# A hybrid decoder trunk on one core: the framework's scheduler orders the instructions by its timeline simulation of all engines in place of its simple one

## The chip, the cores and the metric

The kernel runs on one core of a Trainium2 chip. The core has five engines with an instruction queue each: TensorE (PE, matmuls; its weight loads are PEld in the profile), VectorE (DVE), ScalarE (ACT), GpSimd (POOL) and SyncE (SP, which issues the DMAs). An engine runs its queue in order, and semaphores hold an instruction until those of other engines that it needs are done. The metric is the time of one execution on the device in microseconds; lower is better.

## The reference

A trunk of four layers on 256 tokens of width 1024, in float32. Each layer adds half an FFN, a mixer and half an FFN; the mixer of layer i is i mod 3.

```python
def swiglu(h, w_gu, w_down):
    gate, up = jnp.split(h @ w_gu, 2, axis=-1)
    return (jax.nn.silu(gate) * up) @ w_down

for i in range(DEPTH):                      # DEPTH = 4
    kind, j = i % N_MIXERS, i // N_MIXERS
    x = x + 0.5 * swiglu(rmsnorm(x, ffn1_norm[i]), ffn1_w_gu[i], ffn1_w_down[i])
    h = rmsnorm(x, mix_norm[i])
    if kind == 0:   m = gated_deltanet(h, ...)          # layers 0 and 3
    elif kind == 1: m = stick_breaking_attention(h, ...)  # layer 1
    else:           m = dsa_sparse_attention(h, ...)      # layer 2
    x = x + m
    x = x + 0.5 * swiglu(rmsnorm(x, ffn2_norm[i]), ffn2_w_gu[i], ffn2_w_down[i])
return rmsnorm(x, final_norm)
```

The FFN is 1024 to 2 x 2816 and back. The gated DeltaNet projects to q, k, v, a gate z and two numbers per head, runs a short causal convolution and silu over q, k and v, normalises q and k, and solves, per head and chunk of tokens, a unit lower triangular system (`triangular_solve(lower + eye, rhs)`); a state is carried from chunk to chunk; the result is normalised, multiplied by silu(z) and projected back. Stick-breaking attention has 8 heads and log-sigmoid weights in place of a softmax. The sparse attention scores keys with an indexer, keeps the top 64 for each query and attends to those.

## The kernel before

The activations stay in SBUF with features on the partitions, x as 8 tiles of 128 x 256. Weights come in chunks of 128 x 2048 float32 (1 MB) by DMA. Every product is made of three matmuls in the fp32r type: each weight piece of 128 x 512 is split into a high part `h` (ScalarE, L172) and a low part `l` (VectorE, L173), and so are the activations (`xh`, `xl` at L224 and L225; `ah`, `al` at L201 and L202); `mm3` multiplies h by h, l by h and h by l (all matmuls are at L43, transposes at L56). A tile of an in-projection is 48 such matmuls into one PSUM bank, `bankG`; there are four banks under the tag G and four under the tag A. The ten buffers each of `h` and `l` set how far ahead weights can be split.

The program is written by `Trunk`, stage by stage. `ffn` runs 11 steps of two gate/up chunks and one down chunk. Its norm is folded in late: `norm_in` scales x by the gains, and `rstd` sums the squares (`ones,sq` matmuls), takes the inverse square root on VectorE in three Newton steps (`rs_y`, `rs_t`, L212 to L214), spreads it by two transposes (`ident,rs_y`) and copies it to `rb` (ScalarE, L261). What multiplies a tile by `rb` can start only then.

`gdn` is the DeltaNet stage. Sixteen in-projection tiles (kind 0 keys, 1 values, 2 queries, 3 the gate z; four groups `c` of two heads each) go through TensorE in the order of `gdn_order`. Beside them run generators, which write their next instructions whenever a hand-made clock (`now`, `due`, `pump`) says so: `gates` (exponentials and logarithms on ScalarE, then `E`), `keys(c)` (transposes of `kT`, its norm `rs_y`, `kT x kT`, the matrix `LL`, and then the inverse), `values`, `queries` and `delta(c)`. The inverse of a group doubles its block size in six levels, each of which is a strand of steps that wait for each other:

```python
b1.mm(blk(one(b1.t, r)), Ah[:, r], half(X, 0)[:, r])                                  # XX,LL   PE
nc.vector.tensor_mul(r4(Y), r4(b1.t), lmask[:, lv, None, :].to_broadcast([P, 4, 64]))  # L528   DVE
b2.mm(one(b2.t, r), XT[:, r], one(Y, r))                                              # Y,XX    PE
nc.vector.tensor_sub(half(X, 0), half(X, 0), c4(b2.t))                                # L533   DVE
b3.mm(blk(one(b3.t, r)), X[:, r], self.identh...)                                     # hf,XX   PE
nc.scalar.activation(half(XT, 1), c4(b3.t), AF.Copy)                                  # L538   ACT
```

At its end stand a residual `R` (L546) and two corrections, which give `XF`. `delta` waits for the inverses of all four groups; then follow the output's norm, the gate (L641) and the out-projection (`bankG<-oh`), which adds to x.

`sb` projects v, then q and k head by head, and runs `attend(h)` beside them: scores, absolute value, exp, log (L717 to L719), `sh`/`sl`, the matmuls with `ntri`, exp (L730), `att,v`, and the split of the head's output; `out_proj` takes two heads a chunk. `dsa` has strands of its own (`factor` with `fac`, `index_scores`, `select`, `attend`).

ScalarE's functions lie in table sets. The framework adds a load wherever an operation's function isn't in the set that is loaded by then.

The text of the program isn't yet the order of the queues. The framework's tile scheduler takes the instructions with their dependencies and orders them again for every engine, assigns buffers and sets the semaphores. It is this scheduler that the change concerns.

## Time and profile before

| | before |
|---|---|
| median of 3 runs | 2086.28 us (2080.59 to 2100.09) |
| profiled execution | 2071.74 us, its span 2069.90 us |
| TensorE busy | 2006.7 us (97%) |
| VectorE busy | 1611.2 us (78%) |
| ScalarE busy | 1306.9 us (63%) |
| GpSimd busy | 160.6 us (8%) |
| mean granted TensorE clock | 0.995 |

The profile is one execution; its span goes from the first to the last instruction, and 1.84 us lie around it. Busy times of an engine add up the stretches in which at least one instruction of it runs. The first DeltaNet stage lies at about 188 to 382 us, the stick-breaking stage at 745 to 853 us, the sparse attention at 1228 to 1325 us and the second DeltaNet stage at 1684 to 1883 us; the rest are the eight FFNs.

### The profile page before, as it was taken

The page shows a single profiled execution, that of the slowest core. Times are in us where ns is not written, and L with a number is a line of the kernel's source. Part 1 is how long each engine was busy: PE and PEld are TensorE (multiplying, and loading weights), DVE is VectorE, ACT ScalarE, POOL GpSimd, SP SyncE. Part 2 cuts the span into 40 slices and gives each one's busy share as a digit, 9 for nine tenths or more (in the row PEclk, how much of TensorE's full clock was granted, in tenths as well). Part 3 has the DMA queues.
Part 4 walks back from the last instruction along what each step waited for, and adds up shares of the span by engine and source line. Part 5 has one row for each costly group of instructions (what it writes and reads, how often), then busy time and mean ns, then how long its engine had stood idle before and what let it go on. Part 6 is the DMA issues. An engine that isn't in the chain of part 4 may idle for free.

```text
span 2069.9 us, 43693 instructions
## 1 busy us (share of the span) xinstructions
PE 2006.7 (97%) x17578; PEld 1975.3 (95%) x17578; DVE 1611.2 (78%) x3456; ACT 1306.9 (63%) x2804; POOL 160.6 (8%) x145
## 2 busy tenths in 40 slices
PE   8999899999999999999999998999999998999998
PEld 8999889999999989999999996999999998899998
DVE  7778898866787776877787788877787788988776
ACT  6666776655666666665666664766666667766664
POOL 1001311100000010100010013100010013111000
PEclk9999999999999999999999999999999999999999
DMA  7555223555455554555555542455555542235552
GB/s 260 200 189 182 103 104 127 176 190 185 164 204 197 190 183 146 178 198 196 191 183 201 187 153 79 150 198 201 186 185 202 186 181 105 101 123 181 186 200 86
DMA packets 52619, 353.93 MB, mean 171 GB/s; under 512 B 6976, under 2 KB 7872, under 8 KB 10688
## 3 DMA queue, kind: packets, MB, share of 16 engines
q1 hardware_dynamic: 52128, 350.49, 47.8%
q8 instruction: 137, 2.24, 0.4%
q10 hardware_dynamic: 288, 0.66, 0.1%
q14 instruction: 66, 0.54, 0.1%
HBM read 350.07 MB, written 1.05 MB: 170 GB/s over the span
## 4 chain that ended last, share of the span: by engine, by line
PE 79%; DVE 15%; ACT 4%; issue 2%; POOL 0%; DMA 0%; SPq 0%; ACTq 0%; DVEq 0%; POOLq 0%
PE bankG L43 52%; PE bankA L43 26%; DVE l L173 6%; ACT x L224 1%; PE bankA L56 1%; DVE kT L470 1%; ACT h L172 1%; DVE x L225 1%; DVE rs_t L213 1%; DVE rs_y L214 1%; DVE x L306 1%; DVE rs_t L212 1%; DVE qT L470 0%; DVE e L334 0%; DVE vT L470 0%
## 5 line engine op out<-in xcount | busy, mean ns | idle before, releaser
L43 PE MATMUL bankG<-x,h 128*128 128x256 f32 x7008 | 1256.5, 280 | 10.0 <-ACT x L224 6.8
L173 DVE TENSOR_TENSOR l<-r,h 128x512 fp32r<-128x512 f32 x1328 | 938.2, 713 | 396.7 <-ACT h L172 395.3
L172 ACT ACTIVATE h<-r 128x512 fp32r<-128x512 f32 x1328 | 821.9, 626 | 573.5 <-PE bankG L43 329.6
L43 PEld LDWEIGHTS bankG<-x,h 128*128 128x128 f32 x7008 | 1079.4, 189 | 12.4 <-ACT x L224 7.1
L43 PE MATMUL bankG<-x,l 128*128 128x256 f32 x3504 | 977.5, 279 | 0.0
L43 PEld LDWEIGHTS bankG<-x,l 128*128 128x128 f32 x3504 | 661.9, 189 | 0.2
L43 PE MATMUL bankA<-al,h 128*128 128x256 f32 x1408 | 389.6, 277 | 0.0
L43 PE MATMUL bankA<-ah,h 128*128 128x256 f32 x1408 | 389.6, 277 | 0.0
L43 PE MATMUL bankA<-ah,l 128*128 128x256 f32 x1408 | 389.5, 277 | 0.0
L43 PEld LDWEIGHTS bankA<-al,h 128*128 128x128 f32 x1408 | 265.1, 188 | 0.1
L43 PEld LDWEIGHTS bankA<-ah,h 128*128 128x128 f32 x1408 | 264.3, 188 | 0.1
L43 PEld LDWEIGHTS bankA<-ah,l 128*128 128x128 f32 x1408 | 264.3, 188 | 0.0
L334 DVE TENSOR_TENSOR e<-e,bankG 128x256 f32<-128x256 f32 x352 | 145.3, 413 | 1.8 <-ACT e L333 1.8
L333 ACT ACTIVATE e<-bankG 128x256 f32<-128x256 f32 x352 | 133.7, 380 | 9.1 <-PE bankG L43 8.5
L247 POOL TENSOR_TENSOR sq<-sq 128x512 f32<-128x512 f32 x12 | 15.7, 1304 | 1454.7 <-ACT sq L246 1454.7
L346 DVE TENSOR_TENSOR e<-e,rb 128x512 f32<-128x512 f32 x176 | 119.6, 684 | 0.0
L201 ACT ACTIVATE ah<-e 128x256 fp32r<-128x256 f32 x176 | 72.8, 418 | 23.0 <-DVE e L348 22.7
L347 ACT ACTIVATE e<-e 128x256 f32<-128x256 f32 x176 | 71.2, 405 | 5.8 <-DVE e L346 5.8
L43 PE MATMUL bankG<-oh,h 128*128 128x256 f32 x256 | 73.4, 287 | 0.1
L348 DVE TENSOR_TENSOR e<-e 128x256 f32<-128x256 f32 x176 | 72.8, 418 | 0.5 <-ACT e L347 0.5
L202 DVE TENSOR_TENSOR al<-e,ah 128x256 fp32r<-128x256 f32 x176 | 72.7, 417 | 0.5 <-ACT ah L201 0.5
L43 PE MATMUL bankG<-oh,l 128*128 128x256 f32 x256 | 71.2, 279 | 0.0
(290 smaller groups left out, 1683.7 us busy)
## 6 DMA issues: line engine op xcount, KB each, us to landing
r<-in_ffn SPq DMA_DIRECT2D x262, 1024.0 KB, 4.8
r<-in_gdn_in SPq DMA_DIRECT2D x32, 1024.0 KB, 4.8
r<-in_gdn_out SPq DMA_DIRECT2D x8, 1024.0 KB, 4.7
r<-in_sb_qk SPq DMA_DIRECT2D x8, 1024.0 KB, 4.9
r<-in_sb_v SPq DMA_DIRECT2D x4, 1024.0 KB, 4.8
r<-in_sb_out SPq DMA_DIRECT2D x4, 1024.0 KB, 4.8
r<-in_dsa_out SPq DMA_DIRECT2D x4, 1024.0 KB, 4.8
r<-in_dsa_in SPq DMA_DIRECT2D x3, 1024.0 KB, 4.8
```

Source lines behind the costliest of these rows:

```text
L43: self.nc.tensor.matmul(out, lhsT, rhs, start=self.fresh, stop=stop, skip_group_check=True)
L56: self.nc.tensor.transpose(out, x, self.k.ident)
L172: self.nc.scalar.activation(h[:, :pw], src, AF.Copy)
L173: (self.nc.gpsimd if pool else self.nc.vector).tensor_sub(l[:, :pw], src, h[:, :pw].bitcast(F32))
L201: self.nc.scalar.activation(dh, src, AF.Copy)
L202: self.nc.vector.tensor_sub(dl, src, dh.bitcast(F32))
L212: nc.vector.tensor_mul(t, y, y)
L333: nc.scalar.activation(e[:, m * T:(m + 1) * T], b.t[:, :T], AF.Copy)
L334: nc.vector.tensor_add(e[:, m * T:(m + 1) * T], e[:, m * T:(m + 1) * T], b.t[:, T:])
L346: nc.vector.tensor_mul(e2, e2, st["rb"][:, None, :].to_broadcast([P, 2, T]))
L347: nc.scalar.activation(e[:, :T], e[:, :T], AF.Silu)
L348: nc.vector.tensor_mul(e[:, T:], e[:, T:], e[:, :T])
```

## The change

One argument, in `kernel()`:

```diff
-    with tile.TileContext(nc) as tc:
+    with tile.TileContext(nc, schedule_with_timeline_sim=True) as tc:
         trunk(tc, aps, out)
```

The scheduler now orders the instructions by a timeline simulation of all engines. The instructions of TensorE, VectorE, GpSimd and SyncE are the same. On ScalarE 16 table loads are added, 25 in place of 9: six in each DeltaNet stage, three in the stick-breaking stage and one behind it. Of TensorE's 18086 instructions 6663 stand elsewhere among the others (by up to 832 places), of VectorE's 1622, of ScalarE's 2476 (by at most 80). The middles of the FFNs are as before; what moves lies at the borders of the stages and in the mixers.

In a DeltaNet stage TensorE's in-projection tiles move ahead of the side work: of TensorE's places counted from the start of the program, the `ident,rs_y` transposes for `rb` go from 1684 to 1755, the gates' `gg` matmuls from 1733 to 1870, the first `kT` transposes from 1822 to 2017, the first `hf,XX` matmul of the inverse from 2005 to 2249, and the last of the 16 tiles ends at 2585, where it ended at 3360; the first out-projection matmul goes from 3360 to 3316.

On ScalarE in the first DeltaNet stage, the gates of the first layer before (L420 to L428 are steps of `gates`, each of which waits for the one ahead of it):

```order
L420 ACTIVATE beta<-bankA 128x4x2
L172 ACTIVATE h<-r 128x512
L424 ACTIVATE ge<-gz 128x16
L172 ACTIVATE h<-r 128x512
L425 ACTIVATE ge<-ge 128x16
L426 ACTIVATE ge<-ge,ones 128x16
L428 ACTIVATE ea<-ad 128x8
```

and now:

```order
L420 ACTIVATE beta<-bankA 128x4x2
L172 ACTIVATE h<-r 128x512
L673 ACT_TABLE_LOAD
L673 ACTIVATE z<-z 128x512
L424 ACTIVATE ge<-gz 128x16
L425 ACT_TABLE_LOAD
L425 ACTIVATE ge<-ge 128x16
L172 ACTIVATE h<-r 128x512
L426 ACT_TABLE_LOAD
L426 ACTIVATE ge<-ge,ones 128x16
L428 ACT_TABLE_LOAD
L428 ACTIVATE ea<-ad 128x8
```

The silu of the gate z (L673) has moved between the gates' own steps, and loads of the table sets stand around it; two more follow at the next z, among the exponentials of `E`.

On VectorE in the same stage, the rows up to the last `R` before (`XX` steps are the inverse's, `l` weight splits, `vT` and `pc` the convolution):

```order
L528 TENSOR_TENSOR Y<-bankA,tab 128x256
L173 TENSOR_TENSOR l<-r,h 128x512
L533 TENSOR_TENSOR XX<-XX,bankA 128x8x32
L173 TENSOR_TENSOR l<-r,h 128x512 x2
L459 TENSOR_TENSOR pc_90<-bankG,rb 128x2x256
L528 TENSOR_TENSOR Y<-bankA,tab 128x256
L173 TENSOR_TENSOR l<-r,h 128x512 x2
L533 TENSOR_TENSOR XX<-XX,bankA 128x4x64
L173 TENSOR_TENSOR l<-r,h 128x512
L470 SCALAR_TENSOR_TENSOR vT<-pc_90,conv,vT 128x256 x4
L626 TENSOR_TENSOR a_4758<-qs 128x4
```

and now:

```order
L533 TENSOR_TENSOR XX<-XX,bankA 128x4x64
L528 TENSOR_TENSOR Y<-bankA,tab 128x256
L533 TENSOR_TENSOR XX<-XX,bankA 128x32x8
L546 SCALAR_TENSOR_TENSOR R<-bankA,tab 128x512
L528 TENSOR_TENSOR Y<-bankA,tab 128x256
L533 TENSOR_TENSOR XX<-XX,bankA 128x16x16
L528 TENSOR_TENSOR Y<-bankA,tab 128x256
L533 TENSOR_TENSOR XX<-XX,bankA 128x8x32
L528 TENSOR_TENSOR Y<-bankA,tab 128x256
L533 TENSOR_TENSOR XX<-XX,bankA 128x4x64
L546 SCALAR_TENSOR_TENSOR R<-bankA,tab 128x512
L596 TENSOR_TENSOR u_4658<-bankA,beta 128x256
```

The splits and convolutions that stood between the last group's steps have moved ahead; the steps of the last levels follow each other directly.

On TensorE at the end of the stick-breaking stage, the last head before:

```order
L43 MATMUL bankA<-sl,ntri 128x384
L43 MATMUL bankA<-sp,tab 128x128
L43 MATMUL bankG<-oh,h 128x256
L43 MATMUL bankG<-oh,l 128x256
L43 MATMUL bankG<-ol,h 128x256
L43 MATMUL bankG<-oh,h 128x256
```

(18 out-projection matmuls follow in all before that head's `att,v`, and 60 between `att,v` and the first matmul that reads one of the last two heads) and now:

```order
L43 LDWEIGHTS bf
L43 MATMUL bankA<-bf 128x2x128
L43 MATMUL bankG<-ol,h 128x256 x4
L43 MATMUL bankA<-sh,ntri 128x384
L43 MATMUL bankA<-sl,ntri 128x384
L43 MATMUL bankA<-sp,tab 128x128
L43 MATMUL bankA<-att,v 128x256
L43 MATMUL bankA<-att,v 128x128
L43 MATMUL bankG<-oh,h 128x256
```

`att,v` now follows the `ntri` matmuls directly, and the out-projection matmuls of the last two heads follow `att,v`.

## Rows read from the trace of the kernel before

**Rows 1.** The page: busy time of each engine, and the chain that ended last.

```profile
PE 2006.7 (97%) x17578; PEld 1975.3 (95%) x17578; DVE 1611.2 (78%) x3456; ACT 1306.9 (63%) x2804; POOL 160.6 (8%) x145
...
PE 79%; DVE 15%; ACT 4%; issue 2%; POOL 0%; DMA 0%; SPq 0%; ACTq 0%; DVEq 0%; POOLq 0%
```

**Rows 2.** TensorE's waits, whole span: us in total, times, longest.

```profile
PE bankA L56 <- DVE rs_y L214: 18.3, 18, 2.2
PE bankG L43 <- ACT x L224: 6.8, 2, 6.1
PE bankA L56 <- ACT kT L471: 6.4, 3, 3.1
...
PE bankA L56 <- DVE rs_t L213: 3.8, 2, 2.7
PE bankA L56 <- DVE fac L756: 3.3, 1, 3.3
...
PE bankA L43 <- DVE lat L839: 1.9, 1, 1.9
```

**Rows 3.** Busy time by stretch of the first DeltaNet stage (x: instructions).

```profile
188.00:253.06 65.06, 56.82 (x475) 54.50 (x474) 58.56 (x142) 45.95 (x111) 22.73 (x21) 0.97 0.33 115
253.06:308.74 55.68, 53.33 (x672) 50.55 (x670) 51.86 (x131) 40.80 (x100) 11.35 (x10) 1.00 0.29 102
308.74:382.00 73.26, 70.17 (x616) 69.17 (x615) 65.32 (x187) 49.40 (x135) 10.83 (x10) 1.00 0.35 127
```

**Rows 4.** The chain of waits in that stage, shares by line.

```profile
by line: PE bankG L43 27.5%; DVE l L173 14.5%; PE bankA L43 14.4%; DVE kT L470 4.9%; issue 4.8%; PE bankA L56 3.7%; DVE qT L470 2.6%; ACT x L224 2.3%; ACT h L172 1.8%; DVE vT L470 1.7%; DVE rs_t L213 1.7%; DVE x L225 1.6%; DVE pc L459 1.6%;
```

**Rows 5.** Timeline of the stage: start, us, engine, line, operation [idle before].

```profile
237.83 1.08 PE L56 MATMUL bankA<-ident,rs_y 128*128 128x128 f32 x4 [2.69 <-DVE rs_t L213]
...
253.06 0.61 PE L43 MATMUL bankA<-hf,XX 128*128 128x128 f16 x8
...
259.78 0.29 PE L43 MATMUL bankA<-Y,XX 128*128 128x64 f16 x4
...
260.18 1.24 DVE L533 TENSOR_TENSOR XX<-XX,bankA 128x256 f16<-128x256 f16 x3 [0.34 <-PE bankA L43]
...
261.12 0.29 PE L43 MATMUL bankA<-hf,XX 128*128 128x64 f16 x4
...
308.74 0.68 DVE L546 SCALAR_TENSOR_TENSOR R<-bankA,tab 128x512 f16<-128x512 f32 x1
```

**Rows 6.** Timeline of TensorE in the FFN behind it.

```profile
377.77 0.28 PE L43 MATMUL bankG<-x,l 128*128 128x256 f32 x1
...
378.45 0.28 PE L43 MATMUL bankG<-x,l 128*128 128x256 f32 x1
```

**Rows 7.** VectorE's groups in the stage: busy us, mean ns.

```profile
L173 DVE TENSOR_TENSOR l<-r,h 128x512 fp32r<-128x512 f32 x84 | 63.2, 769 | 5.5 <-ACT h L172 5.4
...
L533 DVE TENSOR_TENSOR XX<-XX,bankA 128x256 f16<-128x256 f16 x24 | 9.8, 414 | 1.6 <-PE bankA L43 1.2
...
L470 DVE SCALAR_TENSOR_TENSOR qT<-pc,conv,qT 128x256 f32<-128x256 f32 x16 | 8.2, 570 | 0.9 <-POOL qT L467 0.9
```

**Rows 8.** ScalarE's groups, whole span, and a table load in its timeline.

```profile
L538 ACT ACTIVATE XX<-bankA 128x256 f16<-128x256 f32 x48 | 16.7, 381 | 16.6 <-PE bankA L43 16.1 <-ACT h L172 0.2
L159 ACT ACT_TABLE_LOAD x9 | 11.5, 1283 | 0.9 <-PEq L1199 0.7
...
219.34 0.63 ACT L449 ACTIVATE E<-E 128x512 f32<-128x512 f32 x1
219.99 1.28 ACT L159 ACT_TABLE_LOAD   x1
221.28 0.63 ACT L471 ACTIVATE kT<-kT 128x512 f32<-128x512 f32 x1
```

**Rows 9.** Two stretches around that wait; PEclk is the third number from the end.

```profile
236.00:238.00 2.00, 0.17 (x1) 0.20 (x2) 2.00 (x10) 2.00 (x6) 0.06 (x1) 0.92 0.94 397
238.00:240.00 2.00, 1.82 (x9) 1.55 (x9) 2.00 (x4) 1.01 (x2) 1.50 (x1) 0.50 0.75 172
```

**Rows 10.** TensorE's waits at one border of two FFNs (560 to 585 us).

```profile
PE bankA L56 <- DVE rs_y L214: 0.7, 1, 0.7
PE bankG L43 <- DVE x L225: 0.2, 1, 0.2
```

**Rows 11.** Stick-breaking stage: TensorE's wait at its start, and the exp of `att`.

```profile
PE bankA L56 <- DVE rs_y L214: 2.2, 1, 2.2
...
L730 ACT ACTIVATE att<-bankA 128x384 f32<-128x384 f32 x8 | 3.9, 489 | 0.4
```

## The prediction

> **What bounds the kernel now.** I read the page's busy times and chain first, then the list of TensorE's waits, then stretches of time, and last the order of the instructions on each engine beside the changed one. TensorE (PE) is busy for 2006.7 of 2069.9 us, and the chain that ended last runs over it for 79% of the span [rows 1]. So every reordering plays for the idle rest, 2069.9 - 2006.7 = 63.2 us, or 3%, and no gain can be larger. The rest lies in few places. In front of VectorE's (DVE's) inverse square roots, `rs_y`, TensorE waits 18.3 us in 18 pieces; 6.8 us are the first weights, which nothing can reorder; 6.4 us are `kT` in the two DeltaNet stages and 3.8 us `rs_t` there [rows 2]. In the middle of an FFN there are almost no waits.
>
> The DeltaNet stage is of another kind. From 188 to 382 us VectorE is busy for 58.56 of 65.06, 51.86 of 55.68 and 65.32 of 73.26 us [rows 3]: 91%, as full as TensorE (180.3 of 194 us). In that stretch the chain steps onto VectorE's weight splits for 14.5% and its convolution for some 8% [rows 4]. Here an order is worth something, and can cost something, because two engines are near their limit and a third strand, the inverse of the four groups of heads, is pure latency.
>
> **The change part by part.** No matmul, VectorE or GpSimd operation is added. What is added is 16 loads of ScalarE's function tables, six in each DeltaNet stage and four in and behind the stick-breaking stage. The rest is order. I take the parts in their places in time, and for each give what I take and both ends.
>
> *DeltaNet, up to the first step of the inverse.* Before, the first `hf,XX` matmul starts at 253.06 us [rows 5], 65 us into the stage. In the changed order TensorE has 244 more instructions ahead of it, nearly all in-projection matmuls. Their pace is six matmuls from 377.77 to 378.45 us [rows 6], so 0.113 us each: 244 x 0.113 = 27.6 us. Against it stand the waits of that part, which now fill up: 65.06 - 56.82 = 8.2 us [rows 3]. By TensorE the step comes 27.6 - 8.2 = 19.4 us later. By VectorE some 30 splits and convolutions more stand ahead, at 0.57 to 0.77 us each [rows 7], 20 us, less its idleness of 65.06 - 58.56 = 6.5 us: 13.5 us. ScalarE's six loads stand in the strand of the gates, which `kT` waits for: 6 x 1.283 = 7.7 us [rows 8], hidden as long as in-projection tiles keep TensorE busy, and they do: there are several tiles between the gate matmuls now. I take +17 us (13.5 to 19.4).
>
> *From there to the last `R`* (the end of the last group's inverse; before, 308.74 us [rows 5], 55.7 us later). One level of the inverse goes TensorE, VectorE, TensorE, VectorE, TensorE, ScalarE. A `Y,XX` at 259.78 is answered by a VectorE operation at 260.18, and the next matmul starts at 261.12 among others' work [rows 5]; with 0.29 us for such a matmul group, 0.42 us for VectorE [rows 7], 0.38 us for ScalarE [rows 8] and about 0.1 us for each of the six handovers, a level takes 0.87 + 0.84 + 0.38 + 0.6 = 2.7 us when nothing is in its way, six levels 16 us, and with the start and the end of the inverse 19 to 22 us. In the order before, the last group began it when VectorE had 27 us of work left to do up to the last `R`, so the latency was covered. In the changed order only 13 us are left, because the splits and convolutions have been done ahead: 42 us of VectorE's work up to the last group's start and then some 22 us of chain, together 64 us against 55.7. I take +9 us (+4 if the chain starts earlier than VectorE's order suggests, +12 if it also queues behind `queries`).
>
> *From the last `R` to the next FFN* (before 73.26 us). Four in-projection tiles, 4 x 48 matmuls x 0.113 = 21.7 us, lay here and now lie ahead. VectorE has about 40 us left in place of 57. So it shortens by 17 to 21.7 us; the delta steps of the last two groups still stand between out-projection matmuls, which gives some back. I take -19 us.
>
> Sum for a stage: 17 + 9 - 19 = +7 us, twice +14 us (ends -3 and +13 for one stage).
>
> *TensorE's clock.* After the wait of 2.69 us at 237.83 [rows 5] the granted clock stands at 0.50 in the next 2 us [rows 9], that is 1.2 GHz; those 2 us did the work of one. With the tiles gone TensorE has only small matmuls between waits for the last 20 us of the inverse. If it falls there, every matmul in it takes twice as long; but most waits there are under 1 us, shorter than that one. I take +1 us a stage, ends 0 and 4: +2 us.
>
> *ScalarE's loads by the skill.* A load in the trace runs from 219.99 to 221.27, the operation ahead of it ends at 219.97 and the one behind starts at 221.28 [rows 8]. The Trainium skill ("ScalarE: Activation LUTs", section on what a table load costs) puts a drain of some 1.38 us beside it, 2.66 us a switch. The trace does not agree: there is no room for it between these rows. By the page's figure the gates' strand would be 6 x 1.38 = 8.3 us longer in each stage and, as an estimate, the time some 10 us above my forecast.
>
> *The borders of the FFNs.* A typical one costs 0.7 us for `rs_y` and 0.2 us for `x` [rows 10]. In the changed order the `rs_y` transposes stand 44 matmuls later, 44 x 0.113 = 5 us, and three or four tiles are advanced together while the x tiles come in. Both waits should go, since TensorE has work it can do. What is late next is the activation of the first tiles, which needs `rb`; I estimate, by the rows' durations along the changed order, that it needs 4 to 7.5 us and has 6.5 to 10. Eight borders at 0.9 us: -7 us (-9 to -3).
>
> *Stick-breaking stage.* Its first wait, 2.2 us [rows 11], shrinks since the v tiles are interleaved: -1.5 us. At its end the last two heads' attention now stands directly in front of the out-projection matmuls that read them. Between the `sh,ntri` matmuls and `att,v` there is nothing left, where 18 out-projection matmuls stood before; what shows is the exp at 0.49 us and a load at 1.28 us [rows 8, 11] with handovers, 2.2 us, then the two splits of the head's output, 0.4 us each with handovers, 1.2 us, and a part of the same for the head ahead of it: +4 us. Net +2.5 us (-1 to +6).
>
> *Sparse-attention stage.* TensorE waits there for `fac` 3.3 us and `lat` 1.9 us [rows 2]; moves are within 55 instructions, and the index scores come some 14 to 39 instructions later, which puts off VectorE's top-k: +1 us (-2 to +5).
>
> Sum: 14 + 2 - 7 + 2.5 + 1 = +12.5 us against the profiled execution's 2071.74 us. That execution was 14.5 us below the median of the runs shown, 2086.28 us, so the difference is what I carry over: **2099 us**, +0.6%.
>
> **The rivals.** *One, faster.* The tiles put ahead close all of TensorE's gaps in the DeltaNet stage, and the end of the stage is set by VectorE's total, which hasn't changed. Then the 13.9 us of idleness of each stage (194.0 - 180.3, [rows 3]) go for the most part, say 8, and the borders' 7: -16 - 7 = -23 us, 2063 us. For it speaks that a simulation of all engines sees exactly these waits; against it that the order shows the last group's inverse with nothing left beside it, and that the latency chain doesn't shrink. It decides from the point at which that group's start is under 30 us behind its place before.
>
> *Two, slower.* The same place, but the price is full: the first inverse step 19.4 us late, the loads in front of `kT` not covered (7.7 us), the chain's 22 us uncovered with the clock at half in it (4 us), the tail shortened by 17 only. That is 19.4 + 4 + 12 + 4 - 17 = +22 us a stage (with half of the loads showing), +44 - 7 + 5 = +42 us, 2128 us. For it speaks that ScalarE's loads stand between the gates' own steps, each waiting for the one before; against it that a tile of TensorE work lies between those steps.
>
> *Three, nothing.* Only 63 us are in play and each place gives and takes: the stages come out within 2 us, the borders' gain shows alone: -3 us, 2083 us. It is not apart from my forecast by what a measurement tells.
>
> **How the numbers follow.** A measurement of this kernel can tell about 1% from no change, so the bounds are 2065 and 2107 us. My forecast has 0.38 and rival three 0.12, both within; rival two has 0.33, taken as anything from +21 us on, and rival one 0.17, anything from -21 us down. The unknown costs, all at their low ends, give -6 - 9 - 1 - 2 = -18 us (2068), and all at their high ends +26 + 8 - 3 + 6 + 5 = +42 us (2128). With rival one's own time at the lower end the range is 2063 to 2128 us; beyond it I leave about a third of each of the outer two.
>
> **What would show it.** In the changed kernel's trace: the first `hf,XX` of the first stage at about 270 us (253 before), the last `R` at about 335 us, the next FFN's start at about 389 us; VectorE idle for about 10 us ahead of the last `R`; 25 table loads at 1.28 us, six of them between the `rb` copy and the first kT silu; no `rs_y` wait at an FFN's border; a wait of 2 to 4 us in front of the last `att,v` matmuls. Wrong it would be if the inverse of the last group starts as early as before, because TensorE's place in the row says little about when it is ready, or if the tiles put ahead run into the weights' buffers and wait for VectorE's splits themselves: then the first part is dearer and the tail not cheaper.

## The result, and the profile after

The changed kernel takes 2149.56 us (median; 2146.06 to 2156.09) against 2085.73 us: a ratio of 1.0347, with an interval of 1.0303 to 1.0392. Ratios here and below are taken over the executions in the fast state and need not be the quotient of the medians beside them, which is 1.0306 here. It is slower by 64 us, where I forecast 13 us and ended the range at 2128.

The page of the changed kernel, busy times and chain, answers to [rows 1]:

```profile
PE 2035.7 (95%) x17578; PEld 1996.3 (93%) x17578; DVE 1628.8 (76%) x3456; ACT 1323.2 (62%) x2820; POOL 158.2 (7%) x145
...
PE 80%; DVE 13%; ACT 5%; issue 2%; DMA 0%; POOL 0%; SPq 0%; DVEq 0%; ACTq 0%; POOLq 0%
```

The span is 2144.3 us, 74.4 us longer than that of the profiled execution before. TensorE's idle time went from 63.2 to 108.6 us, and its busy time rose by 29.0 us although it runs the same matmuls. So about three fifths of the loss are waits, and two fifths are matmuls that took longer. (The execution before holds one FFN that was 6 us slow, of which the last section tells; without it the second part would be 35 us.)

To see where, I cut the span at the last addition into x of each stage (the start of its row in VectorE's timeline, L306; where the row merges two additions, the cut lies up to 0.5 us early). Each stage figure here and below is read from one profiled execution. In us:

| | DeltaNet, layer 0 | stick-breaking | sparse attention | DeltaNet, layer 3 | other FFNs, mean |
|---|---|---|---|---|---|
| before | 183.3 | 107.2 | 112.0 | 183.8 | 181.9 |
| changed | 215.9 | 114.4 | 118.7 | 218.1 | 181.5 |

(The FFNs' mean leaves out the first, and one of 188.3 us before, of which the last section tells.) The DeltaNet stages lost 32.6 and 34.3 us, the two other mixers 7.2 and 6.7, the first FFN 2.3, and each FFN won 0.3.

The first DeltaNet stage of the changed kernel by stretches (columns as in [rows 3]): up to the first `hf,XX`, from there to the last `R`, and from there to the last addition into x.

```profile
195.44:287.79 92.35, 80.09 (x663) 78.12 (x662) 77.27 (x164) 64.77 (x142) 26.02 (x24) 0.94 0.41 149
287.79:348.07 60.28, 51.23 (x619) 47.04 (x618) 48.17 (x124) 39.16 (x96) 9.36 (x8) 0.92 0.20 71
348.07:411.30 63.23, 51.20 (x388) 48.02 (x387) 46.22 (x153) 30.66 (x96) 4.85 (x4) 0.91 0.16 55
```

Before, cut in the same way:

```profile
193.10:253.06 59.96, 51.72 (x430) 49.48 (x429) 53.46 (x129) 42.13 (x103) 22.73 (x21) 0.97 0.32 109
...
308.74:376.40 67.66, 64.95 (x572) 64.15 (x571) 59.94 (x181) 43.97 (x124) 6.54 (x6) 1.00 0.38 137
```

The first stretch is 32.4 us longer, the inverse 4.6 us longer than its 55.68 us [rows 3], and the tail is only 4.4 us shorter, although 184 fewer TensorE instructions lie in it: TensorE is idle for 12.0 us of it, 2.7 us before. The mean clock of the whole stage is 0.93; before it was 0.99.

TensorE's waits in that stage of the changed kernel (190 to 412 us):

```profile
PE bankA L56 <- DVE rs_y L214: 10.4, 3, 6.9
PE bankG L43 <- ACT oh L201: 3.1, 2, 1.6
PE bankA L56 <- DVE rs_t L212: 2.9, 1, 2.9
PE bankA L43 <- DVE kT L496: 2.4, 2, 2.2
PE bankA L43 <- DVE gg L430: 2.4, 1, 2.4
...
PE bankA L43 <- ACT s L601: 2.3, 1, 2.3
PE bankA L56 <- DVE on L633: 1.6, 1, 1.6
PE bankA L43 <- DVE u L615: 1.2, 2, 0.7
```

The wait for `kT` of [rows 2] is gone, and a longer one has come behind it: 6.9 us for `rs_y`, the norms of the third group of keys. ScalarE's timeline in the gates of the changed kernel shows the loads on the strand:

```profile
220.30 1.28 ACT L673 ACT_TABLE_LOAD   x1
221.60 0.63 ACT L673 ACTIVATE z<-z 128x512 f32<-128x512 f32 x1
222.13 0.20 ACT L424 ACTIVATE ge<-gz 128x16 f32<-128x16 f32 x1
222.35 1.28 ACT L425 ACT_TABLE_LOAD   x1
...
224.40 1.28 ACT L426 ACT_TABLE_LOAD   x1
225.69 0.31 ACT L426 ACTIVATE ge<-ge,ones 128x16 f32<-128x16 f32 x1
226.02 1.28 ACT L428 ACT_TABLE_LOAD   x1
...
247.42 0.61 ACT L471 ACTIVATE kT<-kT 128x512 f32<-128x512 f32 x1
```

TensorE's timeline has the start of that strand and its end, the first `hf,XX`; the changed kernel, then the start before:

```profile
216.82 0.38 PE L56 MATMUL bankA<-ident,pad 128*128 128x128 f32 x2
...
275.48 0.28 PE L43 MATMUL bankG<-x,h 128*128 128x256 f32 x1
282.64 1.09 PE L56 MATMUL bankA<-ident,rs_y 128*128 128x128 f32 x4 [6.89 <-DVE rs_y L214]
285.92 2.08 PE L43 MATMUL bankA<-kT 128*128 128x128 f32 x8 [2.19 <-DVE kT L496]
287.79 0.42 PE L43 MATMUL bankA<-hf,XX 128*128 128x128 f16 x2
```

```profile
206.70 0.44 PE L56 MATMUL bankA<-ident,pad 128*128 128x128 f32 x2
```

From the `ident,pad` transposes, where the gates begin, to the first silu of `kT` the changed kernel takes 216.8 to 247.4 us, 30.6; before it took 206.7 to 221.3 [rows 8], 14.6. And the clock (the third number from the end), in four of the six stretches of the stage in which it was low: behind the wait for `gg`, around the one for `rs_y`, within the inverse, and in the tail.

```profile
229.00:233.00 4.00, 4.00 (x21) 4.00 (x22) 2.24 (x6) 1.62 (x5) 0.00 (x0) 0.57 0.74 258
280.00:290.00 10.00, 5.16 (x26) 4.73 (x27) 8.97 (x21) 4.12 (x10) 4.08 (x5) 0.53 0.01 2
345.00:349.00 4.00, 3.48 (x36) 3.09 (x37) 1.54 (x3) 1.44 (x4) 0.00 (x0) 0.57 0.00 0
390.00:400.00 10.00, 5.36 (x24) 4.80 (x25) 6.16 (x29) 2.10 (x9) 0.00 (x0) 0.67 0.01 2
```

All four are at 1.2 GHz for most of their length. In the first TensorE is busy without a gap, at half the pace, behind a wait of 2.4 us. In the third the waits are short; those of 343 to 349 us:

```profile
PE bankA L43 <- DVE XX L533: 1.0, 2, 0.5
PE bankA L43 <- ACT XX L538: 0.7, 1, 0.7
```

### The profile page after: what moved, and what is told of

Same layout as the page of the kernel before. It is cut to its first block, busy times and chain, and to the rows that moved or that the text cites. A ratio compares the mean times of both kernels' runs of the same rounds, so it can differ in the third digit from the quotient of the medians.

```text
span 2144.3 us, 43728 instructions
## 1 busy us (share of the span) xinstructions
PE 2035.7 (95%) x17578; PEld 1996.3 (93%) x17578; DVE 1628.8 (76%) x3456; ACT 1323.2 (62%) x2820; POOL 158.2 (7%) x145
## 4 chain that ended last, share of the span: by engine, by line
PE 80%; DVE 13%; ACT 5%; issue 2%; DMA 0%; POOL 0%; SPq 0%; DVEq 0%; ACTq 0%; POOLq 0%
PE bankG L43 53%; PE bankA L43 26%; DVE l L173 4%; DVE x L225 2%; PE bankA L56 1%; ACT h L172 1%; DVE x L306 1%; ACT junk L622 1%; DVE Y L528 0%; DVE kT L470 0%; DVE rs_t L212 0%; DVE vT L470 0%; DVE rs_t L213 0%; DVE pc L459 0%; DVE XX L533 0%
## 5 line engine op out<-in xcount | busy, mean ns | idle before, releaser
L43 PE MATMUL bankG<-x,h 128*128 128x256 f32 x7008 | 1239.0, 280 | 12.9 <-ACT x L224 6.0
L173 DVE TENSOR_TENSOR l<-r,h 128x512 fp32r<-128x512 f32 x1328 | 929.3, 705 | 408.7 <-ACT h L172 407.3
L172 ACT ACTIVATE h<-r 128x512 fp32r<-128x512 f32 x1328 | 823.1, 626 | 579.5 <-PE bankG L43 337.2
L43 PE MATMUL bankA<-al,h 128*128 128x256 f32 x1408 | 383.2, 277 | 0.0
L43 PE MATMUL bankG<-oh,h 128*128 128x256 f32 x256 | 78.3, 309 | 9.7 <-ACT oh L201 9.7
L43 PE MATMUL bankG<-oh,l 128*128 128x256 f32 x256 | 76.3, 301 | 0.0
L43 PE MATMUL bankG<-ol,h 128*128 128x256 f32 x256 | 71.3, 302 | 0.2 <-DVE ol L202 0.2
```

The source lines that it names most:

```text
L43: self.nc.tensor.matmul(out, lhsT, rhs, start=self.fresh, stop=stop, skip_group_check=True)
L172: self.nc.scalar.activation(h[:, :pw], src, AF.Copy)
L173: (self.nc.gpsimd if pool else self.nc.vector).tensor_sub(l[:, :pw], src, h[:, :pw].bitcast(F32))
```

## The experiments

Stages are cut as above; "before" is run on the same chip each time, and its median was 2080.9 to 2086.6 us. First question: the table loads or the tiles?

**The silu pinned.** The changed kernel with

```diff
-                nc.scalar.activation(gz[c], gz[c], AF.Silu)
+                self.tc.keep_in_program_order(nc.scalar.activation(gz[c], gz[c], AF.Silu))
```

> The changed kernel with the z silu of the DeltaNet stages pinned to its place in the program, so that ScalarE's table loads fall from 25 to 13 (none of them between the gates' steps) while TensorE's tiles stay ahead of the side work as in the changed kernel. Theory A (the loads and the silu between the gates' steps make the strand late): the gates end 8 us earlier in each stage and the waits and the slow clock behind them shrink, 2150 - 2 x 12 = about 2126 us. Theory B (tiles put ahead of the side work leave the inverse bare, whatever the loads do): the 8 us of the gates are swallowed by tiles that stand ahead of the kT transposes anyway, at most 3 us a stage, 2144 us or more.

2142.86 us, ratio 1.0257 (1.0203 to 1.0311); stages of 209.6 and 209.3 us. The 12 loads and the silu's place cost 6.3 and 8.8 us a stage in this order: more than theory B allowed and less than theory A asked, a fifth and a quarter of the stages' loss. (Other instructions move a little with the pin, TensorE's by 5 places on average in the first stage.) Up to the first `hf,XX`:

```profile
203.50:288.55 85.05, 77.54 (x666) 76.04 (x663) 74.48 (x157) 55.35 (x130) 27.61 (x23) 0.97 0.45 162
```

That is 7.3 us less than in the changed kernel.

**Loads in the old order.** The kernel before with `act_set` calls between the gates' steps, two ahead of the first exp, one each ahead of the log and of the exp behind it, and two among the exponentials of `E`.

> The kernel before with six table loads put between the same steps of the gates of each DeltaNet stage (21 loads in all), the order otherwise left to the simple scheduler. Theory A: each load shows, 6 x 1.28 = 7.7 us a stage and some more behind it, 2086 + 2 x 9 = about 2104 us. Theory B: in the old order TensorE has tiles to do meanwhile and VectorE splits, so they show by 3 us a stage at most, 2086 to 2092 us.

2107.01 us, ratio 1.0113 (1.0078 to 1.0148); stages of 197.0 and 198.0 us. That is 14 us a stage. But the loads came out as seven, 9.0 us: an exponential of `E` came between the two that I had written there, and the framework added one (L456; ScalarE's timeline):

```profile
219.52 1.28 ACT L159 ACT_TABLE_LOAD   x1
220.81 1.28 ACT L456 ACT_TABLE_LOAD   x1
222.10 0.63 ACT L456 ACTIVATE E<-E 128x512 f32<-128x512 f32 x1
222.76 1.28 ACT L159 ACT_TABLE_LOAD   x1
```

And the simple scheduler moved others with them: TensorE's instructions stand 8 places off on average in the first stage, 69 at most. That stage as a whole:

```profile
192.97:389.96 196.99, 176.82 (x1670) 170.65 (x1668) 167.05 (x440) 134.71 (x333) 39.60 (x36) 0.94 0.31 109
```

TensorE is idle for 20.2 us of it and busy for 176.8, where it was 13.3 and 170.0 before: half of the 14 us are waits, and half are matmuls that took longer, at a mean clock of 0.94 in place of 0.99. So the strand of the gates isn't hidden in the old order either; how much of the 14 us is the loads' and how much that of the places moved isn't shown.

**Pinned to the program.** Every instruction of an engine in the DeltaNet stages queued behind the one that the program writes before it:

```diff
+PINS = {'gdn': ('PE',)}
...
+            k.pin(at, PINS.get(s[0], ()))
```

The second of the two kernels has `('PE', 'DVE', 'Activation')` there.

> The changed kernel with TensorE's instructions of the two DeltaNet stages held in the program's order; VectorE and ScalarE there, and everything elsewhere, are still ordered by the timeline simulation. The table loads fall to 13 by this. Theory B: both stages come back to within 5 us of the 183 us before, 2150 - 2 x 29 = about 2092 us. Against it (VectorE's splits and convolutions put ahead are the cause, not TensorE's tiles): the stages stay above 200 us, 2120 us or more.

> The changed kernel with TensorE, VectorE and ScalarE held in the program's order in the two DeltaNet stages. What is left of the change is the rest of the program. Both stages within 4 us of before, so what is left above before is +7 us in the stick-breaking stage, +7 in the sparse attention, +2 at the start and -3 at the FFNs' borders: 2086 + 13 = about 2099 us. If the stages stay 15 us or more longer, then the program's order alone is no substitute and the simple scheduler adds something of its own.

2150.99 us (1.0308, 1.0242 to 1.0374; stages of 212.9 and 210.9 us) and 2463.52 us (1.1795, 1.1741 to 1.185; 370.5 and 371.2 us). Both missed, and the premise was wrong: the program's order isn't the order before. In the second kernel TensorE's largest wait tells why (193 to 565 us, which is the first stage; L183 there is L172):

```profile
PE bankG L43 <- ACT h L183: 126.1, 17, 23.7
```

The program writes a tile's weight splits after the side work of the tile before, and the simple scheduler had drawn them ahead. The two kernels tell nothing on the cause. From here on I used the sequences that the kernel before really has.

**Sequences given back.** The numbers of the instructions of one engine, in the order that they have before, are written into the kernel, and each is queued behind its predecessor. What isn't listed stays free.

```diff
+    def queue(self, start, order):
+        here = {i.name: i for i in self.nc.cur_bb.bb.instructions[start:]}
+        for ids in order:
+            seq = [here["I-%d" % n] for n in ids if "I-%d" % n in here]
+            for p, i in zip(seq, seq[1:]):
+                self.tc.add_manual_dep(i, p.name, mybir.DependencyInfo(mybir.DependencyClass.NoSync, mybir.DependencyReason.DATA),
+                                       reason="queue")
```

> The changed kernel, but in the two DeltaNet stages TensorE, VectorE and ScalarE run exactly the sequence that they have in the kernel before; the rest stays as the timeline simulation orders it. If the order of these three queues is the whole cause, both stages take 183 us as before, and what is left above before is the other stages: +7 stick-breaking, +7 to 10 sparse attention, +2 start, -2 borders, 2081 + 15 = about 2096 us. If buffers or semaphores given by the other scheduler matter as well, the stages stay above 190 us each, 2110 us or more.

> The changed kernel, with ScalarE's sequence in the two DeltaNet stages as before (no extra load there); VectorE's then comes out near that of before too, while TensorE's tiles still stand 50 to 70 places ahead of the side work. Theory V (the weight splits and convolutions put ahead on VectorE make the inverse late): stages of 184 to 190 us, about 2105 us. Theory T (the tiles put ahead on TensorE do it): stages of 198 us or more, 2125 us or more.

> As the last, but VectorE's sequence is that of before and ScalarE's is left to the timeline simulation, which puts two of the extra loads and a silu among the exponentials of E. Theory V: stages of 186 to 193 us, that is the last kernel's and 3 us for the two loads, about 2110 us. Theory T: 200 us or more a stage, 2130 us or more.

> The changed kernel with TensorE's sequence in the two DeltaNet stages as before; VectorE and ScalarE are left to the timeline simulation and come out near those of before. It differs from the kernel in which ScalarE's sequence was given back (VectorE and ScalarE near those of before, stages of 217 us) in TensorE's queue alone. If TensorE's order is the cause, the stages take 184 to 188 us, about 2098 us. If not, above 205 us a stage, 2130 us or more.

> The changed kernel with TensorE's and ScalarE's sequences in the DeltaNet stages as before; VectorE's comes out 4 places from that of before on average, 65 at most. If what is left of the loss with TensorE's sequence alone given back (206 us a stage) lies on VectorE, the stages stay at 200 us or more, about 2125 us; if it lies in ScalarE's small differences, they fall to 190 us or less, 2105 us.

> The changed kernel with TensorE's and VectorE's sequences in the DeltaNet stages as before; ScalarE's differs by one place on average and has two loads more a stage among the exponentials of E. If what is left lies on VectorE: 184 + 4 for the loads = 188 us a stage, about 2103 us. If on ScalarE: 200 us or more, 2125 us.

> The changed kernel with VectorE's and ScalarE's sequences in the DeltaNet stages exactly as before and TensorE's left to the timeline simulation, 36 places off on average. If TensorE's place for the tiles costs by itself, 205 us a stage or more, about 2130 us; if the loss needs VectorE's or ScalarE's own moves, 190 us or less, 2105 us.

| sequences as before | us | ratio (interval) | DeltaNet stages |
|---|---|---|---|
| none (the change) | 2149.56 | 1.0347 (1.0303 to 1.0392) | 215.9, 218.1 |
| ScalarE | 2154.18 | 1.0320 (1.0283 to 1.0358) | 217.2, 216.7 |
| VectorE | 2167.12 | 1.0405 (1.0360 to 1.0449) | 220.2, 220.9 |
| VectorE, ScalarE | 2149.53 | 1.0311 (1.0281 to 1.0341) | 215.7, 217.2 |
| TensorE | 2134.65 | 1.0265 (1.0184 to 1.0347) | 206.0, 205.8 |
| TensorE, ScalarE | 2120.57 | 1.0159 (1.0122 to 1.0195) | 201.3, 202.1 |
| TensorE, VectorE | 2106.27 | 1.0108 (1.0079 to 1.0137) | 191.8, 194.9 |
| all three | 2095.48 | 1.0068 (1.0034 to 1.0102) | 184.0, 184.3 |

With all three the two stages are as before, so there the order is the whole cause, and buffers and semaphores are not. Theory V fell with the second and third row, and my sums of 2105 and 2110 us with it; that TensorE's order alone is the cause fell with the fifth, 206 us a stage where I had expected 184 to 188. In the fourth row VectorE and ScalarE run exactly the old sequences, no load is added in the stages, and TensorE's sequence alone loses 32 us. It isn't the changed kernel's own, though: in the first stage it stands some 37 places from the old one on average, the changed kernel's some 183. So the row shows that an order of TensorE alone can cost as much, and not that TensorE's part of the change did. The rows below show that the other two queues can lose too: with TensorE's sequence right, VectorE's leftovers (4 places off on average, 65 at most) cost 17.5 us (201.7 against 184.2, means of both stages), and ScalarE's moves (one place on average, 25 at most) with two loads a stage 9.2 us. The losses aren't additive over engines: 32.3, 17.5 and 9.2 us add up to more than the 32.8 us of the change. That all three make the same strands late is my reading of it.

The first stage of the kernel of the fourth row by stretches, and of the last row:

```profile
194.80:268.60 73.80, 60.46 (x485) 58.09 (x484) 54.81 (x130) 41.44 (x103) 22.86 (x21) 0.88 0.28 101
268.60:332.10 63.50, 56.38 (x657) 51.73 (x655) 50.74 (x131) 39.41 (x99) 11.38 (x9) 0.92 0.22 76
332.10:410.50 78.40, 66.00 (x538) 63.08 (x536) 59.90 (x182) 44.03 (x126) 6.50 (x6) 0.96 0.33 118
```

```profile
195.10:254.40 59.30, 53.06 (x428) 51.16 (x429) 53.62 (x129) 42.12 (x102) 22.96 (x21) 0.94 0.32 111
254.40:309.80 55.40, 53.15 (x671) 50.18 (x669) 51.80 (x131) 40.31 (x100) 11.96 (x10) 1.00 0.28 102
309.80:379.10 69.30, 66.91 (x577) 66.35 (x578) 60.75 (x182) 44.94 (x124) 6.52 (x6) 0.98 0.38 134
```

14.5, 8.1 and 9.1 us longer. In the fourth row's kernel TensorE waits for what its own queue is too early for (194.8 to 410.5 us; its lines stand 8 further: L181 is L173, L479 is L471):

```profile
PE bankG L43 <- DVE l L181: 8.8, 5, 3.1
PE bankA L56 <- ACT kT L479: 7.1, 2, 4.5
PE bankG L43 <- ACT oh L209: 4.5, 2, 3.4
```

A tile drawn ahead stands at TensorE's head and waits for VectorE's splits, and what the strand needs stands behind it; whether that was ready by then isn't shown. The changed kernel doesn't have this wait (0.4 us for `l` in its whole span), for there the splits have moved ahead too.

**Front and rest.** The fourth row's kernel, with TensorE's sequence as before also up to the first step of the inverse, or also from there on:

> VectorE and ScalarE exactly as before in the DeltaNet stages, and of TensorE's sequence the front too, up to the first step of the inverse; the rest of TensorE's sequence there is the timeline simulation's. With TensorE's whole sequence its own the stage takes 216 us: the front was 14.5 us longer, the inverse 8, the tail 9. If the parts add, the front comes back and the stage takes 216 - 14.5 = about 201 us, the kernel about 2120 us. If a late front is what makes the rest late, 190 us or less, 2100 us.

> The opposite: VectorE and ScalarE as before, TensorE's sequence from the first step of the inverse on as before, and its front the timeline simulation's. If the parts add: 184 + 14.5 = about 199 us a stage, 2115 us. If a late front makes the rest late: 210 us or more, 2140 us.

2134.34 us (1.0241, 1.0198 to 1.0285; 206.3 and 204.4 us) and 2111.96 us (1.0148, 1.0110 to 1.0186; 197.2 and 197.9 us). Of TensorE's 32 us the front costs 197.5 - 184.2 = 13.3 and the rest 205.4 - 184.2 = 21.2 (means). The sum is 34.5 against 32.3 measured together: they add (the stages are 4 us above and 1.5 us below the sums of 201 and 199), and a late front isn't what makes the rest slow.

**The tail.** The changed kernel with only the delta and out-projection matmuls in the old sequence among themselves, without and with the silu pinned:

> The changed kernel with only the delta and out-projection matmuls of TensorE put back into the sequence that they have among themselves before (the last two groups' delta steps ahead of the out-projection in place of behind its first 96 matmuls). Theory F (what the tail lacks is work beside the strands, since the tiles are gone): the stages stay within 4 us of 216 us, 2150 us. Theory O (the last groups' strands start too late, behind the out-projection): the tail of 63 us falls by some 10 us a stage, about 2130 us.

> The last kernel with the z silu pinned as well, so without the loads among the gates' steps. Theory F: as the kernel with the silu pinned alone, 209 us a stage, 2143 us. Theory O: 200 us a stage, about 2123 us.

2151.31 us (1.0332, 1.0270 to 1.0394; 218.4 and 214.4) and 2139.94 us (1.0263, 1.0194 to 1.0331; 209.6 and 208.1). No more than 4 us in one stage comes back, and none in the other. It isn't the delta steps' place behind the out-projection, and theory F's sums hold.

**The wrong way round.** The kernel before, under its simple scheduler, with VectorE's sequence of the changed kernel in the DeltaNet stages:

> The kernel before under its simple scheduler, with VectorE's sequence in the two DeltaNet stages as in the changed kernel; TensorE's and ScalarE's then come out as in the changed kernel too, loads included. If the order of the queues is the whole cause there, the stages take 216 us each and the other stages what they took before: 2081 + 66 = about 2147 us. If the timeline scheduler's buffers or semaphores are a part of it, clearly less.

2168.89 us, ratio 1.0388 (1.0340 to 1.0437); stages of 225.2 and 230.7 us. The other scheduler does the same, and worse, if it has to follow that sequence.

**The other stages.** All four mixers in the old sequences, and with the first FFN too:

> The changed kernel with TensorE, VectorE and ScalarE in the sequence of before in all four mixers (so 9 loads again); the timeline simulation orders the FFNs, their borders and the start alone. If the loss outside of the DeltaNet stages lies in the sequences of the stick-breaking and the sparse stage, those come back to 107 and 112 us, and the rest shows the borders' gain: +2 at the start, -0.4 us at each of eight borders, 2081 - 1 = about 2080 us, the same as before. If it lies at the stages' borders, 2090 us or more.

> The changed kernel with the first FFN and all four mixers in the sequences of before on TensorE, VectorE and ScalarE; the timeline simulation orders the other seven FFNs and their borders. The kernel with the mixers alone given back took 2076 us against 2087; the first FFN was 2 to 3 us longer in it than before, which should come back too: 0.994 of the kernel before, about 2073 us on the same scale.

2075.72 us (0.9952, 0.9917 to 0.9987) and 2076.94 us (0.9955, 0.9931 to 0.9980). So the losses of the mixers and of the start are orders as well: 108.7 and 111.9 us for the stick-breaking and the sparse stage in the first, 192.2 us for the first FFN in the second. The timings don't show the start's part: the second kernel gains no more than the first. What is left, the simulation's order at the FFNs' borders, is a gain of some 10 us by the timings, half a per cent, and these two are the only versions that beat the kernel before. The profiles don't show those 10 us (the stages of the first add up to about what they were); part of it may be the scatter of which the last section tells.

## Why the prediction was wrong, step by step

**The front, "I take +17 us (13.5 to 19.4)": 32.4 us.** TensorE's side was priced right: its busy time in this part rose by 28.4 us (80.09 - 51.72), where the additional instructions were put at 27.6. The step that failed is that the waits there "now fill up", -8.2 us, and with it that the loads are "hidden as long as in-projection tiles keep TensorE busy, and they do". The tiles did: TensorE was busy for 81.83 of the first 85 us (190 to 275). But a filler in TensorE's queue doesn't shorten a strand; it only moved the idle time behind it. When the tiles were used up at 275.8 us TensorE had 6.9 us to wait for `rs_y` and 2.2 for `kT`, and its idle time in this part is 12.3 us, 4.0 more than before. Along the strand the 32.4 us are these: it begins 7.8 us later in the stage (`ident,pad`, behind the tiles put ahead), its gates take 16.0 us longer, and the rest up to the first `hf,XX` 8.6. The loads, priced at 7.7 us and then at nothing, are worth 7.3 us of it by the pinned silu; without them TensorE's idle time is still 7.5 us (85.05 - 77.54), as much as before, so the waits don't fill up then either.

**The inverse, "I take +9 us": 4.6 us.** Right in kind and inside the ends; the steps follow each other with little beside them, as forecast. TensorE's idle time in it rose from 2.4 to 9.1 us.

**The tail, "I take -19 us": -4.4 us.** The step that failed is "4 x 48 matmuls x 0.113 = 21.7 us, lay here and now lie ahead. [...] So it shortens by 17 to 21.7 us": I took the tiles out at TensorE's pace, as if it were TensorE's work that sets its length. It was set by the delta strands, which the tiles had covered. With the tiles gone TensorE's idle time in it rose from 2.7 to 12.0 us, and of the waits above those for `oh`, `rs_t`, `s`, `on` and `u`, 11.1 us, lie there, all of them steps of `delta` and of the output. Its busy time fell by 13.8 us only, in part because some of what it did ran at the lower clock. The tail experiments show that the place of the delta steps among the out-projection matmuls doesn't matter then.

**The clock, "I take +1 us a stage, ends 0 and 4": about 10 us.** TensorE is busy for 182.5 us in the first DeltaNet stage (the three rows above added) and 170.0 before, with the same matmuls. The clock stood at 0.50 in six stretches of it, and in one before. The six added up, and the one:

```profile
sum 30.73, PE 23.27 PEld 21.82 DVE 20.69 ACT 11.11 POOL 6.38; mean PE 3.88 PEld 3.64 DVE 3.45 ACT 1.85 POOL 1.06
```

```profile
237.70:241.11 3.41, 3.10 (x14) 2.86 (x15) 3.41 (x9) 1.31 (x3) 2.29 (x2) 0.50 0.80 252
```

At half the pace half of the busy time in them is lost, 11.6 us against 1.6; that makes 10 of the 12.5 us, and the other 2.5 are open. The reason that I gave, most waits being shorter than the one of 2.69 us, was the wrong test: the clock fell behind one wait of 2.4 us at 229 us, and at 345 us it fell with no wait of over 0.73 us in the 20 us ahead. These 12.5 us don't come on top of the three parts above but lie in them: the 32.6 us of the stage are 20.0 us of waits and 12.5 us of busy time.

**The borders, "-7 us (-9 to -3)": -2 us in the profile.** The `rs_y` waits there are gone, as forecast. But the FFNs are shorter by 0.3 us each only, for TensorE now waits for `x` (L225) for 5.9 us in 15 pieces over the span, where it was 3.2 us in 9. The first FFN, which the sum had at nothing, lost 2.3 us.

**Stick-breaking, "+2.5 us (-1 to +6)": +7.2 us. Sparse attention, "+1 us (-2 to +5)": +6.7 us.** In the first the two waits that I named are there; TensorE's waits in it (775 to 890 us):

```profile
PE bankG L43 <- ACT oh L201: 3.1, 2, 2.6
PE bankA L43 <- ACT att L730: 1.9, 1, 1.9
```

TensorE's idle time rose from 2.2 to 5.1 us there, about what I had put for the waits. What the sum left out is busy time, 109.3 us in place of 105.0, with a mean clock of 0.97 against 1.00. In the sparse stage TensorE is busy for 100.1 us both times, and the loss is waits: 4.7 us for `p`, 4.3 for `K` and 2.5 for `rs_y`, where they were 1.4, 0.8 and 0.6. The waits that I named there, for `fac` and `lat`, didn't grow.

Of the rivals, the second came nearest, with an uncovered strand and the clock at half in it, but it put them in the wrong place. In its own terms the front was 19.4 us and 4 for the loads, against 32.4; the inverse 12 and 4 for the clock, against 4.6; the tail -17, against -4.4. Its 22 us a stage were 10 to 12 us too low, and its 2128 us 22. Against it I had held "that a tile of TensorE work lies between those steps", the same step that failed in the front.

Two slips in the working change nothing of this: the ends of a stage's sum, -3 and +13, are -4 and +14 when the parts' ends are added, and the convolution's share in [rows 4] is 9% and not 8%.

The [rows 8] reading of a load stands: the rows above leave no room for a drain behind 1.28 us, and the Trainium skill's 2.66 us a switch ("ScalarE: Activation LUTs", on what a table load costs) isn't seen there. In the changed order they cost about their own 7.7 us a stage, 6.3 and 8.8; in the old order seven of them, 9.0 us, cost 14 with the places that moved.

## What to carry to other kernels

Where two engines are about 90% busy and a strand of small steps runs beside them, as here, bulk work is worth most as cover for the strand: drawn ahead it makes the front look full and leaves the strand bare, and then a wait can cost more than itself (20.0 us of waits came with 12.5 us of longer matmuls in one stage). Price a reordering from the strand's own length, start to end, and not from the places in the fullest engine's queue. Three queues that were good together aren't good one by one, so when a scheduler's order loses, give whole sequences back, two at a time as well, and keep the new order only where it wins (here by half a per cent at most).

## What the runs showed that I had not expected

Some FFNs run 4% slower over their whole length, with no wait and the granted clock at 1.00. In the kernel before, two stretches of 50 us, the first in such an FFN:

```profile
400.00:450.00 50.00, 50.00 (x426) 50.00 (x426) 34.39 (x66) 29.50 (x60) 0.00 (x0) 1.00 0.54 190
600.00:650.00 50.00, 50.00 (x444) 50.00 (x443) 36.20 (x70) 29.97 (x61) 0.00 (x0) 1.00 0.55 197
```

426 matmuls in place of 444: they start 117.8 ns apart in place of 113.3. It is TensorE alone, for ScalarE's and VectorE's weight splits take the same time in both (629 and 628 ns, 689 and 689). Such an FFN takes 187 to 189 us in place of 182. It came in none to three of the eight FFNs of a profiled execution, not always in the same ones, in the old order as in the new; it may be a good part of the scatter of some 20 us between executions (2080.59 to 2100.09 before). Its cause is open.

How fast a strand's delay grows was new too: 9.0 us of loads, with the places that moved beside them, cost 14 us in the old order, and a sequence of ScalarE that differs by one place on average, with two loads, 9 us.
